# An encoder layer in fp32 by Strassen products: weight sums from GpSimd to VectorE, later attention steps, and sums of activations kept in memory

## The chip, the cores and the metric

The kernel runs on one core of a Trainium2 chip. A core has TensorE (PE in the profile), VectorE (DVE), ScalarE (ACT), GpSimd (POOL) and SyncE (SP), whose queue issues all transfers here. The metric is the device time of one execution in microseconds (us); lower is better.

## What is computed

One encoder layer over 1024 + 512 tokens of width 2048. The linear parts take nearly all of the work:

```python
h = rms_norm(x, pre_g)
q, k, v, g_attn, u, vg, g_gmlp = split(h @ w_in)
a = window_attention(rope(q), rope(k), v, sink) * silu(g_attn)
m = spatial_gating(gelu(u), gelu(vg), ln_g, ln_b, ws, bs) * silu(g_gmlp)
y = concat([a, m]) @ w_out
x = x + rms_norm(y, post_g)
x = x + sigmoid(x @ w_pg) * (p @ w_pe)
```

Attention has 8 heads in 2 groups and looks at blocks of 128 tokens, the own one and its neighbours.

## The kernel before

**Products.** The 1536 tokens are two halves of 768, and the depth of 2048 is two halves of 1024, each of eight tiles of 128. Two column blocks of 128 make a pair. For each pair the four quarter products of a 2 x 2 block product are made from seven products of sums (Strassen), numbered 1 to 7. `A_OF` says which quarters of the activations (A) product `pr` uses and with what sign, `B_OF` the same for the weights. Five of the seven have a sign on either side: two quarters have to be added or subtracted first. Every operand is split into a rounded part and the rest (`split_to`: ScalarE rounds, VectorE subtracts), and each product is three matmuls of 128x384 (`mm3`, lines 174 to 176) for each of 8 depth tiles and 2 token chunks: 48 matmuls, called a pass here.

**Sweeps.** Five sweeps follow each other: a and b (parts of `h @ w_in`), c (the gates), y (`w_out`) and p (`w_pg`), with 8, 6, 8, 8 and 8 pairs. Each goes through the products in the order 3, 5, 7, 1, 4, 2, 6, and in each through its pairs. That is 266 passes. a, b and c have the same A, the normed x, stored as `hn`. Tiles carry the sweep, the product and the pair: `wra7_2_01` is a loaded quarter of a weight, `wta7_2` the split weight, `ara7_3` a quarter of A, `aa7_3` its split, `psa7_2` the product in PSUM.

**Weights.** `make_weights` loads one or two quarters of 128x1024, lets GpSimd add or subtract them into the first (`add(G, ...)`, an instruction of line 155 or 158, the helpers `add` and `sub`), and splits it. **A.** `fetch_operand` loads one or two quarters of 128x768 for the next product and lets VectorE add them; `split_operand` splits it as soon as TensorE is through with the old tile of the same place, so eight splits come in the last pass of a product. For product 7 of sweep a, `x1_normed` makes the sum from tiles that it norms at that time. **Leaving.** `leave_product` adds a product into the accumulators of the pair (VectorE, from PSUM, sometimes ScalarE); only then can the PSUM tile, one of two, take the pass after next. The results then go through rotary steps (`rope`: VectorE and GpSimd), gelu, gates and stores.

**Beside the sweeps.** `embed` makes `p @ w_pe` first, whose 32 products `leave_pe` copies out of PSUM with VectorE. Attention runs as 24 jobs in between (`attention`, half of them in sweep b, half in c): scores `s`, exponentials, transposes `t` of the probabilities `p`, their split `pt`, the output `o`. Spatial gating (`mixing`) lies between the halves.

**Order.** Each engine runs its instructions in the order in which the program issues them. `Line` sets this order: every job is a generator, `yield us` says when it wants to go on, counted on a clock that TensorE's planned time moves (`line.spend`), and between TensorE's steps the jobs that are due issue their instructions. A larger number after `yield` puts what follows later in every queue; nothing waits for a time on the chip. The SP queue is in order too: a store that waits holds the loads behind it.

```python
heapq.heappush(self.jobs, (max(self.now - 1.5, due) + wait, c, gen))
```

Of the kernel before, what the change touches and what calls it, by code (L numbers as in the profile page):

```python
# [9 lines left out]
F32 = mybir.dt.float32  # L10
# [89 lines left out]
def tile_encoder_layer(ctx: ExitStack, tc: tile.TileContext, xT, pT, wall, pre_g, post_g, sink,  # L100
# [69 lines left out]
    def halves(t):  # L170
        return t.rearrange("p (c x) -> p c x", c=2)
# [40 lines left out]

    weights, raw, operands, passes = {}, {}, {}, [0]

    def make_weights(j, sw, pr, i):

        nm = f"{sw.name}{pr}_{i}"
        sign, *quarters = B_OF[pr]
        rs = []
        for kh, n in quarters:  # L220
            r = wrp.tile([P, 1024], F32, tag="wr", name=f"wr{nm}_{n}{kh}")
            load_w(r, sw.pairs[i][n][0], kh)
            rs.append(r)
        yield 9.0
        if sign:
            (add if sign > 0 else sub)(G, rs[0], rs[0], rs[1])
            yield 3.5
        yield from when(lambda: passes[0] >= j - 2)
        w = wtp.tile([P, 2, 1024], F32R, tag="wt", name=f"wt{nm}")
        yield from split_to(rs[0], w[:, 0, :], w[:, 1, :])  # L230
        weights[j] = w

    def fetch_operand(s, sw, pr, k):

        nm = f"{sw.name}{pr}_{k}"
        if s == 1:
            yield from when(lambda: x_stored[0] > 8 + k)
        sign, *quarters = A_OF[pr]
        rs = []
        for pool, tag, (th, kh) in zip((arp, wk), ("ar", "wk"), quarters):  # L240
            r = pool.tile([P, HT], F32, tag=tag, name=f"ar{nm}_{th}{kh}")
            load(r, sw.a[th][kh][k])
            rs.append(r)
        if sign:
            yield 9.0
            (add if sign > 0 else sub)(V, rs[0], rs[0], rs[1])
        raw[s, k] = rs[0]

    def split_operand(s, sw, pr, k):
        yield from when(lambda: (s, k) in raw)  # L250
# [143 lines left out]

    def leave_pe(j, h, ps):
        o = arp.tile([P, HT], F32, tag="ar", name=f"pe{j}_{h}")
        V.tensor_copy(out=halves(o), in_=ps[:, :, 0:CH])
        yield 1.6
        store(pe_d[j][h], o)

# [178 lines left out]
    def attend_qk(g, n, into):  # L579
        b0, b1 = span_of(n)  # L580
        w = (b1 - b0) * P
        nm = f"{g}_{n}"
        h, off = n // HB, (n % HB) * P
        r = [work(f"aq{nm}"), work(f"ak{nm}")]
        load(r[0][:, 0:512].rearrange("p (i t) -> p i t", i=4),
             q_d[g][h][:, :, off:off + P].rearrange("i p t -> p i t"))
        load(r[1][:, 0:w], k_d[g][:, b0 * P:b1 * P])
        yield 9.0
        q = four(f"qs{nm}", [P, 2, 512], F32R)
        ks = four(f"ks{nm}", [P, 2, 512], F32R)  # L590
        nc.scalar.activation(q[:, 0, :], r[0][:, 0:512], AF.Copy)
        nc.scalar.activation(ks[:, 0, 0:w], r[1][:, 0:w], AF.Copy)
        yield 0.8
        sub(V, q[:, 1, :], r[0][:, 0:512], q[:, 0, :].bitcast(F32))
        yield 0.6
        sub(V, ks[:, 1, 0:w], r[1][:, 0:w], ks[:, 0, 0:w].bitcast(F32))
        yield 3.0
        into.append((q, ks))

    def attend_v(g, n, into):  # L600
# [11 lines left out]
    def attend(g, n, got):  # L612

        b0, b1 = span_of(n)
        m0 = (b0 - n + 1) * P
        nb = b1 - b0
        w = nb * P
        nm = f"{g}_{n}"
        h, off = n // HB, (n % HB) * P
        yield from when(lambda: got)  # L620
        q, ks = got.pop()
        mx = small.tile([P, 4], F32, tag="mx", name=f"mx{nm}")
        sm = small.tile([P, 4], F32, tag="sm", name=f"sm{nm}")
        es = small.tile([P, 4], F32, tag="es", name=f"es{nm}")
        gv = []
        line.spawn(attend_v(g, n, gv), 1.0)
        ss, ps_ = [], []

        def reduce(i):
            hd = 4 * g + i  # L630
            p = pp.tile([P, 3 * P], F32, tag="p", name=f"p{nm}_{i}")
            V.tensor_tensor_reduce(out=p[:, 0:w], in0=ss[i][:, 0:w], in1=mask_sb[:, m0:m0 + w],
                                   op0=ALU.add, op1=ALU.min, scale=-SCALE,
                                   scalar=nsink[:, hd:hd + 1], accum_out=mx[:, i:i + 1])
            ps_.append(p)

        def expo(i):
            nc.scalar.activation(ps_[i][:, 0:w], ps_[i][:, 0:w], AF.Exp, scale=-1.0, bias=mx[:, i:i + 1],
                                 accum_out=sm[:, i:i + 1])

        for i in range(6):
            if i < 4:
                ss.append(side(f"s{nm}_{i}"))
                mm3(ss[i][:, 0:w], [q[:, x, i * P:(i + 1) * P] for x in range(2)],
                    [ks[:, x, 0:w] for x in range(2)], True, True, w / 2400. + 0.0133)
            if 1 <= i < 5:
                reduce(i - 1)
            if i >= 2:
                expo(i - 2)
            yield 1.0  # L650
        add(V, es, mx, sink_sb[:, 4 * g:4 * g + 4])
        yield 0.3
        nc.scalar.activation(es, es, AF.Exp)
        yield 0.6
        add(V, sm, sm, es)
        V.reciprocal(out=sm, in_=sm)
        yield 0.6
        for i in range(4):
            nc.scalar.activation(ps_[i][:, 0:w], ps_[i][:, 0:w], AF.Copy, scale=sm[:, i:i + 1])
        yield 4.6  # L660
        pts = {}

        def turn(b):
            tp = side(f"t{nm}_{b}")
            for i in range(4):
                nc.tensor.transpose(tp[:, i * P:(i + 1) * P], ps_[i][:, b * P:(b + 1) * P], ident)
            line.spend(0.43)
            yield 0.4
            pt = pts[b] = four(f"pt{nm}_{b}", [P, 2, 512], F32R)
            yield from split_to(tp, pt[:, 0, :], pt[:, 1, :], 0.9)  # L670

        def weigh(b):
            mm3(o, [vs[:, x, b * P:(b + 1) * P] for x in range(2)],
                [pts[b][:, x, :] for x in range(2)], b == 0, b == nb - 1, 0.2266)

        yield from turn(0)
        yield from turn(1)
        yield from when(lambda: gv)
        vs = gv[0]
        yield 2.0  # L680
        o = side(f"o{nm}")
        weigh(0)
        if nb > 2:
            yield from turn(2)
            yield 2.0
        for b in range(1, nb):
            weigh(b)
        yield 0.8
        t = work(f"ao{nm}")
        nc.scalar.activation(t[:, 0:512], o, AF.Copy)  # L690
        yield 1.5
        store(at_d[g][h][:, :, off:off + P].rearrange("i p t -> p i t"),
              t[:, 0:512].rearrange("p (i t) -> p i t", i=4))
        attended.add((g, n))
# [128 lines left out]
    def x1_normed(k):  # L823
# [9 lines left out]
        if k >= 8:  # L833
            sub(V, r, r, t)
            raw[2, k - 8] = r
        store(hn[1][k // 8][k % 8], t)

    for k in range(KT):
        along("a", 3, k // 2, x1_squares(k), 4.0 * (k % 2))
# [156 lines left out]
```

## Time and profile before

| | us |
|---|---|
| median of 3 runs | 2557.67 (2557.42 to 2560.88) |
| the profiled execution | 2555.26 |
| its span, first to last instruction | 2553.5 |
| TensorE busy | 2483.7 |
| VectorE busy | 1731.8 |
| ScalarE busy | 966.0 |
| GpSimd busy | 708.1 |

Transfers move 645.97 MB, nearly all by one queue. A wait in the profile is named by the engine that waits, the tile and line of the waiting instruction, and behind `<-` what ended last before it began. A stretch 50:125 is from 50 to 125 us after the first instruction. The granted clock is TensorE's, 1.00 being 2.4 GHz.

### The profile page before, as it was taken

How to read it: one execution, taken by the hardware profiler on the slowest of the kernel's cores; microseconds unless marked ns; L12 is line 12 of the kernel's file. 1: busy time of each engine (PE TensorE's matmuls, PEld its weight loads, DVE VectorE, ACT ScalarE, POOL GpSimd, SP SyncE). 2: the span in 40 equal slices, each digit the busy share in tenths (PEclk: the TensorE clock that was granted, in tenths of full speed). 3: DMA queues.
4: the chain of work that ended last, by engine and by line, in shares of the span. 5: the costliest groups of instructions: out<-in, count | busy, mean ns of one | idle time of the engine just before them, and what ended most of it. 6: DMA issues, size and time to landing. Idle time of an engine off the chain costs nothing.

```text
span 2553.5 us, 36547 instructions
## 1 busy us (share of the span) xinstructions
PE 2483.7 (97%) x14268; PEld 2448.7 (96%) x14268; DVE 1731.8 (68%) x1903; ACT 966.0 (38%) x1386; POOL 708.1 (28%) x300
## 2 busy tenths in 40 slices
PE   7999999999999999999998899999999999999999
PEld 7898999999989999999998899999999999999998
DVE  7659566866676767667767665556577976757775
ACT  3243222224775543333546742332233333322421
POOL 0254334454022102301221013203220331433444
PEclk9999999999999999999999999999999999999999
DMA  8957776667566688878656577567577988879985
GB/s 292 387 197 262 249 238 230 225 211 263 195 225 212 180 270 293 303 248 300 200 173 209 187 273 280 219 215 250 170 245 257 342 313 305 302 251 301 325 315 208
DMA packets 372397, 645.97 MB, mean 253 GB/s; under 512 B 29312, under 2 KB 212096, under 8 KB 372224
## 3 DMA queue, kind: packets, MB, share of 16 engines
q1 hardware_dynamic: 372224, 643.63, 73.9%
q8 instruction: 112, 1.84, 0.3%
q14 instruction: 61, 0.50, 0.1%
HBM read 533.43 MB, written 110.10 MB: 252 GB/s over the span
## 4 chain that ended last, share of the span: by engine, by line
PE 80%; DVE 9%; ACT 4%; issue 3%; DMA 3%; POOL 1%; SPq 1%; DVEq 0%; POOLq 0%; ACTq 0%
PE psy L175 6%; PE psy L176 6%; PE psy L174 6%; PE psp L175 6%; PE psp L176 6%; PE psp L174 6%; PE psc L176 4%; PE psc L174 4%; PE psc L175 4%; PE psa L175 4%; PE psa L176 4%; PE psa L174 4%; PE psb L175 4%; PE psb L176 4%; PE psb L174 4%
## 5 line engine op out<-in xcount | busy, mean ns | idle before, releaser
L174 PE MATMUL psa<-aa,wta 128*128 128x384 f32 x896 | 302.3, 337 | 5.7 <-DVE oa L155 3.8
L175 PE MATMUL psa<-aa,wta 128*128 128x384 f32 x896 | 301.7, 337 | 6.0 <-DVE aa L158 5.9
L176 PE MATMUL psa<-aa,wta 128*128 128x384 f32 x896 | 301.1, 336 | 5.8 <-DVE wta L158 5.8
L174 PE MATMUL psc<-ac,wtc 128*128 128x384 f32 x896 | 305.5, 341 | 0.0
L174 PE MATMUL psp<-ap,wtp 128*128 128x384 f32 x896 | 300.5, 335 | 3.2 <-ACT ap L166 2.6
L175 PE MATMUL psp<-ap,wtp 128*128 128x384 f32 x896 | 300.5, 335 | 2.4 <-DVE ap L158 2.4
L175 PE MATMUL psc<-ac,wtc 128*128 128x384 f32 x896 | 301.4, 336 | 0.3 <-DVE ac L158 0.3
L176 PE MATMUL psc<-ac,wtc 128*128 128x384 f32 x896 | 300.7, 336 | 0.0
L176 PE MATMUL psp<-ap,wtp 128*128 128x384 f32 x896 | 299.9, 335 | 0.0
L174 PE MATMUL psy<-ay,wty 128*128 128x384 f32 x896 | 299.6, 334 | 0.0
L176 PE MATMUL psy<-ay,wty 128*128 128x384 f32 x896 | 299.3, 334 | 0.0
L175 PE MATMUL psy<-ay,wty 128*128 128x384 f32 x896 | 299.3, 334 | 0.0
L174 PE MATMUL psb<-ab,wtb 128*128 128x384 f32 x672 | 231.2, 344 | 0.5 <-DVE ua L155 0.5
L175 PE MATMUL psb<-ab,wtb 128*128 128x384 f32 x672 | 226.4, 337 | 2.7 <-DVE ab L158 2.7
L176 PE MATMUL psb<-ab,wtb 128*128 128x384 f32 x672 | 226.0, 336 | 0.0
L175 PEld LDWEIGHTS psa<-aa,wta 128*128 128x128 f32 x896 | 169.3, 189 | 8.4 <-DVE aa L158 8.3
L174 PEld LDWEIGHTS psa<-aa,wta 128*128 128x128 f32 x896 | 169.5, 189 | 6.7 <-issue 4.1
L176 PEld LDWEIGHTS psa<-aa,wta 128*128 128x128 f32 x896 | 169.5, 189 | 6.1 <-DVE wta L158 6.1
L174 PEld LDWEIGHTS psp<-ap,wtp 128*128 128x128 f32 x896 | 168.6, 188 | 4.0 <-ACT ap L166 2.9
L175 PEld LDWEIGHTS psp<-ap,wtp 128*128 128x128 f32 x896 | 168.7, 188 | 3.9 <-DVE ap L158 3.6
L175 PEld LDWEIGHTS psc<-ac,wtc 128*128 128x128 f32 x896 | 169.2, 189 | 1.6 <-DVE ac L158 1.0
L174 PEld LDWEIGHTS psc<-ac,wtc 128*128 128x128 f32 x896 | 169.5, 189 | 0.5
(257 smaller groups left out, 5429.8 us busy)
## 6 DMA issues: line engine op xcount, KB each, us to landing
wrc<-wall SPq DMA_DIRECT2D x96, 512.0 KB, 6.5
arb<-h SPq DMA_DIRECT2D x96, 384.0 KB, 5.9
arc<-h SPq DMA_DIRECT2D x96, 384.0 KB, 6.0
wry<-wall SPq DMA_DIRECT2D x72, 512.0 KB, 6.2
wrp<-wall SPq DMA_DIRECT2D x72, 512.0 KB, 6.8
arp<-x SPq DMA_DIRECT2D x88, 384.0 KB, 6.5
wra<-wall SPq DMA_DIRECT2D x60, 512.0 KB, 5.9
ara<-h SPq DMA_DIRECT2D x80, 384.0 KB, 5.9
```

The lines of the kernel that those rows point to most:

```text
L174: nc.tensor.matmul(ps, lhsT=l[0], rhs=r[0], start=start, stop=False)
L175: nc.tensor.matmul(ps, lhsT=l[0], rhs=r[1], start=False, stop=False)
L176: nc.tensor.matmul(ps, lhsT=l[1], rhs=r[0], start=False, stop=stop)
```

## The change

It does four things. `make_weights` adds or subtracts weight quarters on VectorE (`V`) and not on GpSimd (`G`), and counts 1.6 us and not 3.5 for it. The sums of A that sweep a makes (five products, eight tiles of 128x768 each) are stored to memory (`sum_d`), by `fetch_operand` or, for product 7, by `x1_normed`, and sweeps b and c load such a sum where they loaded two quarters and added them. `leave_pe` copies its first half with ScalarE. In the attention, what follows the split of q and k comes 1.0 later, what follows the scaling of the probabilities 1.0 later, and the two places before the output's matmuls 1.2 later.

```diff
--- before.py
+++ after.py
@@ -212,6 +212,8 @@
 
     weights, raw, operands, passes = {}, {}, {}, [0]
 
+    sum_d = {pr: [scratch(f"sum{pr}_{k}", [P, HT]) for k in range(8)] for pr in A_OF if A_OF[pr][0]}
+
     def make_weights(j, sw, pr, i):
 
         nm = f"{sw.name}{pr}_{i}"
@@ -223,8 +225,8 @@
             rs.append(r)
         yield 9.0
         if sign:
-            (add if sign > 0 else sub)(G, rs[0], rs[0], rs[1])
-            yield 3.5
+            (add if sign > 0 else sub)(V, rs[0], rs[0], rs[1])
+            yield 1.6
         yield from when(lambda: passes[0] >= j - 2)
         w = wtp.tile([P, 2, 1024], F32R, tag="wt", name=f"wt{nm}")
         yield from split_to(rs[0], w[:, 0, :], w[:, 1, :])
@@ -236,6 +238,11 @@
         if s == 1:
             yield from when(lambda: x_stored[0] > 8 + k)
         sign, *quarters = A_OF[pr]
+        if sign and sw.name in "bc":
+            r = arp.tile([P, HT], F32, tag="ar", name=f"ar{nm}")
+            load(r, sum_d[pr][k])
+            raw[s, k] = r
+            return
         rs = []
         for pool, tag, (th, kh) in zip((arp, wk), ("ar", "wk"), quarters):
             r = pool.tile([P, HT], F32, tag=tag, name=f"ar{nm}_{th}{kh}")
@@ -245,6 +252,9 @@
             yield 9.0
             (add if sign > 0 else sub)(V, rs[0], rs[0], rs[1])
         raw[s, k] = rs[0]
+        if sign and sw.name == "a":
+            yield 1.5
+            store(sum_d[pr][k], rs[0])
 
     def split_operand(s, sw, pr, k):
         yield from when(lambda: (s, k) in raw)
@@ -394,7 +404,10 @@
 
     def leave_pe(j, h, ps):
         o = arp.tile([P, HT], F32, tag="ar", name=f"pe{j}_{h}")
-        V.tensor_copy(out=halves(o), in_=ps[:, :, 0:CH])
+        if h:
+            V.tensor_copy(out=halves(o), in_=ps[:, :, 0:CH])
+        else:
+            nc.scalar.activation(halves(o), ps[:, :, 0:CH], AF.Copy)
         yield 1.6
         store(pe_d[j][h], o)
 
@@ -594,7 +607,7 @@
         sub(V, q[:, 1, :], r[0][:, 0:512], q[:, 0, :].bitcast(F32))
         yield 0.6
         sub(V, ks[:, 1, 0:w], r[1][:, 0:w], ks[:, 0, 0:w].bitcast(F32))
-        yield 3.0
+        yield 4.0
         into.append((q, ks))
 
     def attend_v(g, n, into):
@@ -657,7 +670,7 @@
         yield 0.6
         for i in range(4):
             nc.scalar.activation(ps_[i][:, 0:w], ps_[i][:, 0:w], AF.Copy, scale=sm[:, i:i + 1])
-        yield 4.6
+        yield 5.6
         pts = {}
 
         def turn(b):
@@ -677,12 +690,12 @@
         yield from turn(1)
         yield from when(lambda: gv)
         vs = gv[0]
-        yield 2.0
+        yield 3.2
         o = side(f"o{nm}")
         weigh(0)
         if nb > 2:
             yield from turn(2)
-            yield 2.0
+            yield 3.2
         for b in range(1, nb):
             weigh(b)
         yield 0.8
@@ -834,6 +847,9 @@
             sub(V, r, r, t)
             raw[2, k - 8] = r
         store(hn[1][k // 8][k % 8], t)
+        if k >= 8:
+            yield 1.5
+            store(sum_d[7][k - 8], r)
 
     for k in range(KT):
         along("a", 3, k // 2, x1_squares(k), 4.0 * (k % 2))
```

How the built order changes is shown at three places, all on VectorE. In each, the first excerpt is of the kernel before and the second of the changed one.

Sweep a's start, product 3, around the split of pass 2's weight (`wta3_2`); `ara5_0` to `ara5_2` are sums of A for product 5, `aa3_6` is a split of A:

```order
L158 TENSOR_TENSOR aa3_6_1060<-x0_6_345,aa3_6_1060 128x768
L155 TENSOR_TENSOR ara5_0_00_1065<-ara5_0_00_1065,ara5_0_01_1067 128x768
L155 TENSOR_TENSOR ara5_1_00_1101<-ara5_1_00_1101,ara5_1_01_1103 128x768
L158 TENSOR_TENSOR wta3_2_1173<-wra3_2_10_1042,wta3_2_1173 128x1024
L158 TENSOR_TENSOR wta3_3_1184<-wra3_3_10_1076,wta3_3_1184 128x1024
L155 TENSOR_TENSOR ara5_2_00_1137<-ara5_2_00_1137,ara5_2_01_1139 128x768
```

The changed kernel at the same place:

```order
L158 TENSOR_TENSOR aa3_6_1100<-x0_6_385,aa3_6_1100 128x768
L158 TENSOR_TENSOR wra3_2_10_1082<-wra3_2_10_1082,wra3_2_11_1084 128x1024
L155 TENSOR_TENSOR ara5_0_00_1105<-ara5_0_00_1105,ara5_0_01_1107 128x768
L158 TENSOR_TENSOR wra3_3_10_1116<-wra3_3_10_1116,wra3_3_11_1118 128x1024
L158 TENSOR_TENSOR wta3_2_1199<-wra3_2_10_1082,wta3_2_1199 128x1024
L158 TENSOR_TENSOR wta3_3_1212<-wra3_3_10_1116,wta3_3_1212 128x1024
L155 TENSOR_TENSOR ara5_1_00_1141<-ara5_1_00_1141,ara5_1_01_1143 128x768
```

The subtractions of the weights of passes 2 and 3 now stand in the row, and the split of `wta3_2` stands ahead of the sum `ara5_1` and not behind it.

The start of sweep p, product 3, while sweep y's last passes leave (`uy_7`); `x7_0` is the last tile of A that the first pass needs, `ap3_7` its split, and `accy1` sums squares for the next norm:

```order
L158 TENSOR_TENSOR wtp3_1_18468<-wrp3_1_10_18352,wtp3_1_18468 128x1024
L158 TENSOR_TENSOR ap3_5_18477<-x5_0_18266,ap3_5_18477 128x768
L158 TENSOR_TENSOR ap3_6_18487<-x6_0_18335,ap3_6_18487 128x768
L155 TENSOR_TENSOR uy_7_15104<-uy_7_15104,psy6_7_18407 128x768
L862 SCALAR_TENSOR_TENSOR y7_0_18403<-y7_0_18403,post_sb_105,rb_y0_17445 128x768
L155 TENSOR_TENSOR x7_0_18404<-x7_0_18404,y7_0_18403 128x768
L155 TENSOR_TENSOR accy1_17381<-accy1_17381,sqyy15_1_18509 128x768
L158 TENSOR_TENSOR ap3_7_18526<-x7_0_18404,ap3_7_18526 128x768
L158 TENSOR_TENSOR wtp3_2_18551<-wrp3_2_10_18423,wtp3_2_18551 128x1024
```

The changed kernel at the same place:

```order
L158 TENSOR_TENSOR wtp3_1_18292<-wrp3_1_10_18192,wtp3_1_18292 128x1024
L158 TENSOR_TENSOR ap3_3_18298<-x3_0_17968,ap3_3_18298 128x768
L158 TENSOR_TENSOR ap3_4_18309<-x4_0_18037,ap3_4_18309 128x768
L158 TENSOR_TENSOR ap3_5_18318<-x5_0_18106,ap3_5_18318 128x768
L158 TENSOR_TENSOR ap3_6_18327<-x6_0_18175,ap3_6_18327 128x768
L155 TENSOR_TENSOR uy_7_14944<-uy_7_14944,psy6_7_18247 128x768
L878 SCALAR_TENSOR_TENSOR y7_0_18243<-y7_0_18243,post_sb_145,rb_y0_17285 128x768
L158 TENSOR_TENSOR wrp3_2_10_18263<-wrp3_2_10_18263,wrp3_2_11_18265 128x1024
L155 TENSOR_TENSOR x7_0_18244<-x7_0_18244,y7_0_18243 128x768
L155 TENSOR_TENSOR accy1_17221<-accy1_17221,sqyy15_1_18349 128x768
L158 TENSOR_TENSOR ap3_7_18366<-x7_0_18244,ap3_7_18366 128x768
L158 TENSOR_TENSOR wtp3_2_18377<-wrp3_2_10_18263,wtp3_2_18377 128x1024
```

A subtraction for pass 2's weight has come in between `y7_0` and `x7_0`, and the split of `wtp3_1` stands further ahead of `ap3_6`.

A stretch of even work, sweep a's product 1, pass 2 of which leaves PSUM with two adds (`va_2`, `ua_2`):

```order
L158 TENSOR_TENSOR wta1_4_2985<-wra1_4_00_2890,wta1_4_2985 128x1024
L155 TENSOR_TENSOR va_2_1881<-va_2_1881,psa1_2_2940 128x768
L155 TENSOR_TENSOR ua_2_1281<-ua_2_1281,psa1_2_2940 128x768
L440 SCALAR_TENSOR_TENSOR xb2_2938<-xb2_2938,pre_sb_104,rb_x1_1823 128x768
L158 TENSOR_TENSOR wta1_5_3053<-wra1_5_00_2955,wta1_5_3053 128x1024
```

The changed kernel at the same place:

```order
L155 TENSOR_TENSOR wra1_4_00_2954<-wra1_4_00_2954,wra1_4_11_2956 128x1024
L158 TENSOR_TENSOR wta1_4_3040<-wra1_4_00_2954,wta1_4_3040 128x1024
L155 TENSOR_TENSOR va_2_1929<-va_2_1929,psa1_2_3004 128x768
L155 TENSOR_TENSOR ua_2_1324<-ua_2_1324,psa1_2_3004 128x768
L453 SCALAR_TENSOR_TENSOR xb2_3002<-xb2_3002,pre_sb_144,rb_x1_1871 128x768
L155 TENSOR_TENSOR wra1_5_00_3019<-wra1_5_00_3019,wra1_5_11_3021 128x1024
L158 TENSOR_TENSOR wta1_5_3106<-wra1_5_00_3019,wta1_5_3106 128x1024
```

The sums of two weight quarters for `wta1_4` and `wta1_5` (`wra1_4`, `wra1_5`) have come in, each directly ahead of the split of the same weight.

## Rows read from the trace of the kernel before

**Rows 1.** The page's busy times of the engines, share of the span, instructions.
```profile
PE 2483.7 (97%) x14268; PEld 2448.7 (96%) x14268; DVE 1731.8 (68%) x1903; ACT 966.0 (38%) x1386; POOL 708.1 (28%) x300
```

**Rows 2.** TensorE's waits: us in total, times, longest us.
```profile
PE o L175 <- DVE pt L158: 8.0, 5, 3.9
...
PE t L666 <- ACT p L659: 7.7, 20, 1.8
...
PE pspe L174 <- DVE pe L397: 5.9, 3, 3.3
...
PE psa L176 <- DVE wta L158: 5.8, 1, 5.8
...
PE s L175 <- DVE ks L158: 5.3, 5, 1.8
...
PE o L174 <- ACT pt L166: 2.2, 1, 2.2
```

**Rows 3.** Busy us and instructions by stretch, granted clock, transfers.
```profile
core 0: us, PE busy (x) PEld busy (x) DVE busy (x) ACT busy (x) POOL busy (x), PEclk, DMA share, GB/s
...
50.00:125.00 75.00, 65.92 (x352) 64.55 (x351) 52.46 (x52) 18.68 (x22) 19.09 (x8) 0.91 0.98 359
...
125.00:200.00 75.00, 74.15 (x431) 73.27 (x430) 38.41 (x32) 32.66 (x42) 38.27 (x18) 1.00 0.60 198
...
200.00:275.00 75.00, 67.38 (x371) 66.05 (x370) 64.67 (x49) 19.65 (x23) 36.89 (x14) 0.95 0.87 300
...
525.00:625.00 100.00, 95.53 (x545) 93.58 (x545) 64.01 (x73) 31.00 (x48) 49.42 (x26) 0.98 0.71 237
...
625.00:900.00 275.00, 268.41 (x1542) 258.82 (x1540) 187.55 (x296) 175.89 (x317) 45.23 (x19) 0.99 0.66 209
...
1350.00:1475.00 125.00, 108.76 (x586) 100.60 (x585) 85.40 (x124) 85.47 (x138) 12.10 (x5) 0.97 0.58 194
...
2050.00:2100.00 50.00, 46.12 (x256) 44.70 (x255) 37.55 (x35) 15.99 (x20) 14.77 (x6) 0.97 0.84 309
...
2300.00:2500.00 200.00, 199.12 (x1149) 198.80 (x1148) 150.24 (x133) 62.70 (x73) 81.16 (x32) 1.00 0.90 311
```

**Rows 4.** Timeline, VectorE and GpSimd, 2064 to 2078 us: start, us.
```profile
2064.27 0.96 DVE L158 TENSOR_TENSOR ap<-x,ap 128x768 fp32r<-128x768 f32 x1
...
2066.48 2.76 POOL L158 TENSOR_TENSOR wrp<-wrp,wrp 128x1024 f32<-128x1024 f32 x1 [4.60 <-DMA wrp<-wall]
...
2066.89 3.17 DVE L158 TENSOR_TENSOR ap<-x,ap 128x768 fp32r<-128x768 f32 x1
...
2073.95 2.98 POOL L158 TENSOR_TENSOR wrp<-wrp,wrp 128x1024 f32<-128x1024 f32 x1 [4.70 <-DVE wtp L158]
...
2074.59 3.15 DVE L158 TENSOR_TENSOR ap<-x,ap 128x768 fp32r<-128x768 f32 x1
```

**Rows 5.** Groups of instructions: count, busy us, mean ns, idle before them.
```profile
L155 POOL TENSOR_TENSOR wrp<-wrp,wrp 128x1024 f32<-128x1024 f32 x24 | 60.6, 2526 | 85.3 <-DMA wrp<-wall 85.3
...
L158 DVE TENSOR_TENSOR wty<-wry,wty 128x1024 fp32r<-128x1024 f32 x56 | 88.6, 1582 | 24.5 <-ACT wty L166 24.5
...
L155 DVE TENSOR_TENSOR arb<-arb,arb 128x768 f32<-128x768 f32 x24 | 23.4, 974 | 1.5 <-DMA arb<-h 1.5
...
L397 DVE COPY pe<-pspe 128x768 f32<-128x768 f32 x32 | 30.5, 953 | 8.1 <-PE pspe L176 7.0 <-DMA wra<-wall 1.1
...
L260 ACT ACTIVATE ua<-psa 128x768 f32<-128x768 f32 x8 | 6.5, 810 | 19.2 <-PE psa L176 19.2
```

**Rows 6.** Timeline, GpSimd and VectorE, 110 to 117 us.
```profile
110.13 2.36 POOL L158 TENSOR_TENSOR wra<-wra,wra 128x1024 f32<-128x1024 f32 x1 [5.33 <-DMA wra<-wall]
...
114.02 1.41 DVE L155 TENSOR_TENSOR ara<-ara,ara 128x768 f32<-128x768 f32 x1 [7.55 <-DMA ara<-h]
...
115.35 1.21 DVE L158 TENSOR_TENSOR wta<-wra,wta 128x1024 fp32r<-128x1024 f32 x1
```

## The prediction

> **What bounds the kernel now.** Read the busy times first: TensorE is busy 2483.7 of 2553.5 us, VectorE 68%, GpSimd 28% [rows 1]. So TensorE sets the end, and only the 69.8 us in which it stands still, and stretches in which it runs at its lower clock, can be won. The table by stretches says where they lie [rows 3]. Idle time is a stretch's width less TensorE's busy time; the clock's share is its width times what the granted clock lacks of 1.00 (full is 2.4 GHz, and a stretch at 1.2 GHz counts half). This gives 9.1 + 6.8 us in 50:125, 7.6 + 3.8 in 200:275, 4.5 + 2.0 in 525:625, 6.6 + 2.8 in 625:900, 16.2 + 3.8 in 1350:1475 and 3.9 + 1.5 in 2050:2100: 47.9 us of idle time and 20.7 of clock. Elsewhere TensorE hardly waits, and what the change adds there has to stay under a pass, 48 matmuls: 200 us / 1149 x 48 = 8.36 us in the stretch 2300:2500 [rows 3]. Last, TensorE's own waits by releaser [rows 2]: the attention's steps (o, t, s) wait 8.0 + 7.7 + 5.3 + 2.2 = 23.2 us, almost always for VectorE or for ScalarE behind it. VectorE is thus the engine that is late where TensorE waits, though it is 68% busy on average.
>
> **Why VectorE is late.** A split of an operand takes 0.96 us. Two splits of the same tile and shape take 3.17 and 3.15 us, and each began while GpSimd ran a weight sum: from 2066.48 for 2.76 us, and from 2073.95 for 2.98 us [rows 4]. The first split ends at 2070.06, 0.82 us after GpSimd's end: VectorE did not share, it stood still until GpSimd was through. The group of all splits of sweep y's weights averages 1.58 us, where 1.21 is the time of one alone [rows 5, 6].
>
> **The weight sums move to VectorE.** There are five signed products of seven and 38 pairs, so 190 sums. GpSimd loses 190 x about 2.6 us [rows 5], some 500 of its 708. VectorE gains 190 x 1.21 = 230 us (a subtraction of two 128x1024 tiles took 1.21 [rows 6]). Three things come off it: 80 sums of A at 0.97 (`arb`) = 78 us [rows 5], 16 copies out of PSUM at 0.95 = 15 us [rows 5], and the standstill behind sums. The last I bound by 0 and 190 x 2.2 us (3.17 - 0.96) and take at 120: not every sum meets a blocked instruction. VectorE ends at 1732 + 230 - 78 - 15 - 120, about 1750 us: as busy as before, but without 2 us holes, and a weight is summed in 1.2 instead of 2.6 us.
>
> What it adds is a wait on VectorE. In 72 of the 190 places the new order puts a weight's split directly behind its sum, as in the third pair of the order's excerpts, and the split needs ScalarE's rounding in between. ScalarE's copies of a smaller tile take 0.81 [rows 5]; scaled to 1024 columns that is 1.08, about 1.2 with both hand-overs. Behind the waiting split stand the adds that empty PSUM for the pass after next. In the densest steady stretch, 2300:2500, VectorE has 150.2 us in 24 passes, 6.26 a pass. With 5/7 x (1.21 + 1.2) = 1.72 more it has 7.98, under 8.36 even if nothing of the standstill goes. So I cost this at little: 3 us in all for new waits, two the size of the one that I leave at sweep p's start, with 0 and 13 us as ends.
>
> **Start, 50:125.** TensorE waits 5.8 us for the split of pass 2's weight [rows 2], which begins at 115.35 because the second operand sum before it waits for its load until 114.02. In the new order the split stands ahead of that sum, behind the subtraction for pass 3, whose load had landed at 110.13 [rows 6]. It then ends at 110.13 + 1.21 + 1.21 = 112.55 instead of 116.56: 4.0 us. The longest wait for a copy out of PSUM, 3.3 us [rows 2], which the move of half the copies to ScalarE should end, brings no more: transfers run at 98% in 50:125, so TensorE would only reach the later wait sooner. ScalarE's 16 copies, 13 us, are hidden beside TensorE; without that cover they would cost 0.81 us each. Against it stand the new stores: 40 of 384 KB, the first eight between the loads of this stage. At 359 GB/s each takes 1.1 us, 8.8 for eight; in 125:200 the share is down to 60%, so I take 4.0, with a loss of 4.8 (4.0 - 8.8) as the other end. The SP queue is in order, and a store waits for its sum; queued behind it are loads of later weights. The other 32 stores lie in stretches with spare transfer time. In sweeps b and c, 80 loads less take 31 MB off.
>
> **Sweep a, 200:275.** VectorE is busy 64.7 of 75 us. Four sums of 7's weights fall here. Each gives back up to 2.2 and costs 1.21, so 1.0 a piece: 4 of the 11.4 us, the ends 0 and 11.4. The rotary steps stay on GpSimd and go on blocking.
>
> **525:625.** GpSimd is busy 49.4 of 100 us with rotary steps and sums in one queue; a sum on VectorE no longer queues behind them. I take 4 of 6.5, ends 0 and 6.5. Here a rule of the Trainium skill speaks against the change: SBUF — State Buffer, section "Who interferes with whom", says that a VectorE instruction with two SBUF inputs contends with a GpSimd instruction that reads SBUF, and that the later one blocks entirely. By it the sums, now such instructions, are themselves held by the rotary steps; this term would be 1 and the total 3 us later, inside the forecast's own range. The pair of splits above agrees with the rule; for a sum on VectorE no run here shows it.
>
> **Attention, 625:900 and 1350:1475.** The allowances grow by 1.0 (before s), 1.0 (before t) and twice 1.2 us (before o): TensorE does other passes meanwhile, at no cost but a later end of the job, and the built order has the last job end in sweep c's second-last product, ahead of the one that needs it. They take at most 1.0 from each of 5 waits of s, 1.0 from each of some 5 jobs with waits of t (20 rows, four in a job), 1.2 from each of 6 of o: 17 us. What is longer than its allowance (3.9, 2.2, 1.8, 1.8) is about what one or two standstills of 2.2 make. I take 16 of the 23.2 and 4 of the clock's 6.6: 20 us, with 0 and 29.8 as ends.
>
> **Start of sweep p, 2050:2100.** Both standstills of 2.2 us lie ahead of the last splits; one sum of 1.21 comes in there (second pair of excerpts). VectorE reaches the last split about 3 us sooner; 4 of 5.4 us.
>
> **Sum.** 4 + 4 + 4 + 20 + 4 - 3 = 33 us. The profiled execution took 2555.26, so 2522; the median of the runs lies 2.4 above it, so **2524 us**.
>
> **Rivals.**
> 1. *Attention stays late.* ScalarE, with its table loads, could be what holds the steps, and the allowances only move the waits. For it: t waits for ScalarE's p in all 20 rows [rows 2]. Against: ScalarE is itself behind VectorE's row there. That term falls from 20 to 6: 2538.
> 2. *Everything is cleared.* All losses of the five later stretches go, 11.4 + 6.5 + 9.4 + 20.0 + 5.4, and 4.0 at the start: 57 us, 2501. Against: the hand-overs still bring eight splits in one pass.
> 3. *Slower: late weights hold VectorE.* On GpSimd a sum that waited for its load held only sums. On VectorE it holds PSUM's emptying and the splits. Place: sweep p and the end of y, where transfers run at 84 to 90% [rows 3]. With a wait of w a sum, a pass takes 7.98 + 0.71 w on VectorE, so it decides from w = 0.5 us; at 2.4 us (a GpSimd sum's whole length lost, the nearest row) it is 1.3 us a pass, over some 54 passes 72 us: 2596. Against: loads are issued 9 us ahead in the program, and its order leaves that as it was.
>
> **Chances.** Forecast 0.60 (2512 to 2536), attention stays late 0.16, all cleared 0.08, late weights 0.10; the other 0.06 is gains and new waits that cancel. Within 0.2%, 5 us, a measurement of this kernel can't tell from no change. So faster 0.84, same 0.06, slower 0.10. The range 2503 to 2548 holds the forecast, the first rival with 10 us on top for the stores' worse end, and stops short of the last.
>
> **What would show it.** GpSimd near 210 us with 110 instructions; VectorE near 1750 with 1997; the weight splits' mean near 1.21; TensorE's idle time near 45 us; pass 2's weight split ending about 4 us sooner; waits for o, t and s together under 8 us. Wrong would be: VectorE idle on weight loads for over 100 us (rival 3), t's waits unchanged (rival 1), a granted clock under 0.90 in 100:200 (the stores).

## The result and the profile after

The changed kernel takes **2497.25 us** (median of four runs, 2496.87 to 2498.64); the kernel before, beside it on the same chip, 2557.55 (2556.95 to 2560.88). The ratio is 0.9763, 95% interval 0.9746 to 0.978. The gain is 60 us where 33 were forecast, and the time lies under the range (2503). The profiled execution took 2496.87 us, its span is 2495.1.

The page's busy times after, in the form of [rows 1]:

```profile
PE 2460.8 (99%) x14268; PEld 2437.8 (98%) x14268; DVE 1704.0 (68%) x1997; ACT 980.6 (39%) x1400; POOL 221.6 (9%) x110
```

TensorE stands still for 2495.1 - 2460.8 = 34.3 us where it stood 69.8. It is also busy 22.9 us less at the same 14268 matmuls: a matmul that runs at the lower clock counts as busy time, and so does a short wait inside a group, since the records overlap (in the rows of transposes further down, 256 of 273 ns each fill 38.9 us). The gain of 58.4 us in the span is thus 35.5 of idle time and 22.9 of busy time.

TensorE's own waits after, answering [rows 2] (engine, tile, line, what ended the wait; us in total, times, longest):

```profile
PE pspe L174 <- ACT pe L410: 4.3, 2, 3.3
PE psa L176 <- DVE wta L158: 3.2, 1, 3.2
...
PE psa L175 <- DVE aa L158: 2.4, 2, 1.5
PE o L175 <- DVE pt L158: 2.1, 3, 1.0
...
PE o L174 <- ACT pt L166: 1.1, 1, 1.1
...
PE s L175 <- DVE ks L158: 0.5, 1, 0.5
PE t L679 <- ACT p L672: 0.4, 2, 0.2
```

The attention's steps (o, t, s) wait 4.1 us, before 23.2. The wait for pass 2's weight has fallen from 5.8 to 3.2.

The stretches of [rows 3] after. The same work stands up to 58 us earlier now, so a stretch shows the idle time and clock of that part of the program, not the same instructions:

```profile
core 0: us, PE busy (x) PEld busy (x) DVE busy (x) ACT busy (x) POOL busy (x), PEclk, DMA share, GB/s
50.00:125.00 75.00, 69.81 (x387) 68.20 (x386) 50.13 (x49) 26.17 (x33) 8.07 (x4) 0.98 1.01 367
...
200.00:275.00 75.00, 70.67 (x397) 70.12 (x397) 63.30 (x55) 20.28 (x24) 17.15 (x7) 0.98 1.00 350
...
525.00:625.00 100.00, 100.00 (x588) 99.64 (x587) 63.09 (x83) 38.06 (x65) 26.10 (x13) 1.00 0.63 207
625.00:900.00 275.00, 272.45 (x1587) 265.12 (x1587) 177.21 (x286) 181.32 (x317) 0.00 (x0) 1.00 0.58 177
...
1350.00:1475.00 125.00, 123.67 (x722) 120.52 (x721) 79.33 (x135) 87.89 (x148) 0.00 (x0) 1.00 0.63 210
...
2050.00:2100.00 50.00, 50.00 (x290) 50.00 (x289) 30.70 (x32) 17.12 (x20) 0.00 (x0) 1.00 0.79 298
```

The groups of weight splits in sweeps y and p, answering [rows 5] (count; busy us, mean ns; idle before), and a split of `x` at sweep p's start, answering [rows 4] (GpSimd ran nothing from 2005 to 2030 us):

```profile
L158 DVE TENSOR_TENSOR wtp<-wrp,wtp 128x1024 fp32r<-128x1024 f32 x56 | 90.2, 1611 | 23.5 <-ACT wtp L166 23.5
...
L158 DVE TENSOR_TENSOR wty<-wry,wty 128x1024 fp32r<-128x1024 f32 x56 | 68.5, 1224 | 42.7 <-ACT wty L166 42.6
```

```profile
2012.81 0.95 DVE L158 TENSOR_TENSOR ap<-x,ap 128x768 fp32r<-128x768 f32 x1
```

Sweep y's splits took 1582 ns before. Sweep p's still have GpSimd's last adds beside them. In the table of stretches, from 525 us on hardly anything is left; what remains lies in the start and around 200 to 275 us.

**Where the gain arose.** The best measure is the start of the same pass in both traces: how much sooner it begins, and by how much that grows from one place of the program to the next. The columns of the two tables below are six pieces of the program: the *start* (up to the first pass of sweep a's product 5, 167.7 us in the kernel before), *a5-7* (up to the fifth pass of product 7, 283.1), *a rest* (up to the second pass of sweep b, 605.6), *attention* (up to sweep y, 1601.9), *y-p3* (up to sweep p's product 5, 2145.9) and *end* (up to the last pass, 2538.7).

| us | start | a5-7 | a rest | attention | y-p3 | end |
|---|---|---|---|---|---|---|
| forecast | 4.0 | 4 | 4 | 20 | 4 | -3 (new waits) |
| measured | 6.4 | 4.6 | 10.1 | 31.4 | 3.9 | 1.7 |

### The profile page after: what moved, and what is told of

Read it like the earlier page. It is cut to its first block, busy times and chain, and to the rows that moved or that the text cites. A ratio compares the mean times of both kernels' runs of the same rounds, so it can differ in the third digit from the quotient of the medians.

```text
span 2495.1 us, 36057 instructions
## 1 busy us (share of the span) xinstructions
PE 2460.8 (99%) x14268; PEld 2437.8 (98%) x14268; DVE 1704.0 (68%) x1997; ACT 980.6 (39%) x1400; POOL 221.6 (9%) x110
## 4 chain that ended last, share of the span: by engine, by line
PE 90%; DVE 3%; DMA 2%; ACT 2%; issue 1%; POOL 0%; SPq 0%; DVEq 0%; ACTq 0%
PE psp L175 6%; PE psp L176 6%; PE psp L174 6%; PE psy L175 6%; PE psy L174 6%; PE psy L176 6%; PE psc L175 6%; PE psc L174 6%; PE psc L176 6%; PE psa L176 5%; PE psa L175 5%; PE psa L174 5%; PE psb L175 4%; PE psb L176 4%; PE psb L174 4%; PE t L679 1%
```

## The experiments

Theory 1: the main loss was VectorE's standstill behind GpSimd's sums. Theory 2: the attention's steps were due too early, whatever GpSimd did. Theory 3: the stored sums relieved VectorE and the transfers. Theory 4 came later. The medians and gains by piece (gain over the kernel before, from one profiled execution each; these scatter between kernels that should agree there, in the start by up to 5 us and in a5-7 by up to 3, so that only larger differences are read; the kernels were timed in six groups, each beside the kernel before, whose median lay between 2556.16 and 2560.35):

| kernel | median us (lowest to highest) | start | a5-7 | a rest | attention | y-p3 | end |
|---|---|---|---|---|---|---|---|
| changed | 2497.25 (2496.87 to 2498.64) | 6.4 | 4.6 | 10.1 | 31.4 | 3.9 | 1.7 |
| e1 changed, sums on GpSimd | 2534.9 (2532.7 to 2539.07) | 3.4 | 2.1 | -1.1 | 18.3 | -2.4 | 0.2 |
| e2 before, sums on VectorE | 2515.22 (2514.17 to 2516.8) | 7.8 | 2.9 | 10.1 | 14.3 | 3.8 | 1.7 |
| e3 before, later attention | 2540.94 (2530.08 to 2544.28) | 0.5 | -1.3 | 0.1 | 18.1 | -0.1 | -1.5 |
| e4 changed, old attention | 2513.33 (2512.8 to 2515.78) | 8.9 | 2.2 | 10.1 | 15.1 | 3.9 | 1.6 |
| e5 before, stored sums | 2555.2 (2549.52 to 2561.53) | 0.2 | 1.1 | -1.6 | 0.4 | -0.4 | -1.0 |
| e6 changed, no stored sums | 2500.4 (2498.99 to 2501.69) | 7.4 | 4.7 | 10.1 | 28.2 | 3.9 | 1.7 |
| e7 before, copies on ScalarE | 2557.71 (2551.12 to 2563.17) | 2.7 | 1.1 | -1.0 | 2.2 | 0.0 | -0.9 |
| e8 changed, old copies | 2498.18 (2497.55 to 2498.65) | 6.3 | 2.9 | 10.1 | 31.5 | 3.9 | 1.6 |
| e9 changed, idle GpSimd adds | 2528.52 (2527.51 to 2530.65) | 8.6 | -4.4 | 2.5 | 27.6 | -6.2 | -3.6 |
| e10 changed, idle GpSimd fills | 2497.26 (2496.61 to 2501.85) | 3.6 | 2.3 | 10.1 | 31.5 | 3.9 | 1.7 |
| e11 changed, no GpSimd sums | 2492.98 (2489.88 to 2495.97) | 8.2 | 9.8 | 10.1 | 31.4 | 3.9 | 1.7 |
| e12 e11, attention later still | 2503.2 (2498.34 to 2504.43) | 8.3 | 8.4 | 10.1 | 23.5 | -0.8 | 1.6 |
| e13 e4, idle GpSimd adds | 2546.61 (2541.79 to 2551.51) | 7.4 | -4.4 | 2.5 | 9.0 | -7.3 | -3.8 |
| e14 changed, sums counted 3.5 | 2509.22 (2502.7 to 2510.21) | 0.3 | 2.5 | 10.0 | 29.6 | 0.7 | 1.6 |

### Two parts of the change, each taken back and each alone (e1 to e4)

The edit of e1, and the reverse of it in the kernel before for e2:

```diff
-            (add if sign > 0 else sub)(V, rs[0], rs[0], rs[1])
-            yield 1.6
+            (add if sign > 0 else sub)(G, rs[0], rs[0], rs[1])
+            yield 3.5
```

> The changed kernel with its 190 weight sums back on GpSimd and their old allowance of 3.5; the stored sums, the copies and the later attention stay. Theory 1 (VectorE standing still while a GpSimd sum runs was the main loss): most of the 60 us comes back, about 2535 us; TensorE waits for o, t and s 10 us or more, the mean of sweep y's weight splits is again near 1.58 us. Theory 2 (the attention's steps were simply due too early): only the stretches outside the attention lose, about 2518 us, and o, t and s stay near 4 us. Theory 3 (the stored sums relieved VectorE and the transfers): under 2510 us.

> The kernel before with one change, the weight sums on VectorE (allowance 1.6). Theory 1: about 2512 us, since without the standstills the old allowances of the attention nearly do. Theory 2: about 2530 us, the attention's waits for o, t and s stay at 20 us or more. Theory 3: no gain or a loss, 2550 us or more, because VectorE then has the 230 us of weight sums and still the 78 us of sums of A.

The four longer allowances in the kernel before (e3), and taken back in the changed one (e4):

```diff
         sub(V, ks[:, 1, 0:w], r[1][:, 0:w], ks[:, 0, 0:w].bitcast(F32))
-        yield 3.0
+        yield 4.0
...
-        yield 4.6
+        yield 5.6
         pts = {}
...
         vs = gv[0]
-        yield 2.0
+        yield 3.2
...
             yield from turn(2)
-            yield 2.0
+            yield 3.2
```

> The kernel before with one change, the four longer allowances in the attention. Theory 1: about 2545 us, o, t and s fall from 23 to some 15 us, since a standstill of 2.2 us and more is longer than the 1.0 to 1.2 us added. Theory 2: about 2528 us, o, t and s under 6 us.

> The changed kernel with the attention's old allowances. Theory 1: about 2505 us, o, t and s at 8 us or less. Theory 2: about 2525 us, o, t and s back at 20 us or more.

Measured: 2534.9, 2515.22, 2540.94 and 2513.33 us. The sums alone gain 41.7 us (2556.93 beside it), the later attention alone 16.0; taken back, they cost 37.7 and 16.1. The two add up to nearly all of the 60. Theory 1 gives the larger part, and the smaller part is theory 2's: neither was right alone. Their signs lie between them too: o, t and s together wait 9.2 us in e3 and 13.6 in e4. In e1 one sign of theory 1 is missing, since sweep y's weight splits average 1.31 us and not 1.58. In the attention both count, 14.3 and 18.1 us, and 14.3 + 18.1 is about the 31.4 of both together. TensorE's waits there in e2 (sums alone) and e3 (later steps alone):

```profile
PE t L666 <- ACT p L659: 5.0, 17, 1.0
PE o L175 <- DVE pt L158: 4.4, 4, 1.6
...
PE o L174 <- ACT pt L166: 2.4, 2, 2.2
...
PE s L175 <- DVE ks L158: 0.8, 1, 0.8
```

```profile
PE o L175 <- DVE pt L158: 6.2, 4, 2.3
...
PE o L174 <- ACT pt L166: 2.1, 2, 1.1
...
PE t L666 <- ACT p L659: 0.9, 5, 0.2
```

Against [rows 2], moving the sums clears s (5.3 to 0.8) and leaves many short waits of t (17, the longest 1.0). The later steps clear t and s and leave the long waits of o. So the two overlap in s and differ in t and o: in the list of waits they take 10.6 and 14.0 us, and 19.1 together. That the gains in time add up so nearly is in part chance; what the list does not hold is busy time, told below.

### The stored sums and the copies (e5 to e8)

For e5 and e6 all lines with `sum_d` are put into the kernel before or taken out of the changed one; for e7 and e8 the branch in `leave_pe`.

> The kernel before with one change, the stored sums of A. Theory 1 (transfers and VectorE's 78 us of sums are hidden, except in the start): a loss at the start up to 5 us, none later, so 2555 to 2560 us; VectorE near 1640 us busy with no gain in time. Theory 3 (they relieve VectorE in the attention, where TensorE waits for it): 2550 us or less.

> The changed kernel without the stored sums: sweeps b and c load two quarters and add them again, VectorE near 1785 us busy. Theory 1: 2493 to 2499 us, at the start some 2 to 5 us better than the changed kernel (no stores between the loads there), later passes equal. Theory 3: 2505 us or more.

> The kernel before with one change, half of the copies out of PSUM at the start on ScalarE. By the prediction (transfers bound the start, TensorE only reaches the later wait sooner): within 1 us of before, about 2557 us. By what the passes of the changed kernel show (sweep a's first pass begins 3.8 us earlier): about 2554 us.

> The changed kernel with all copies at the start on VectorE. By the prediction: 2496 to 2498 us, no change. By the first pass of sweep a, which begins 3.8 us earlier than before in the changed kernel: about 2501 us.

Measured: 2555.2 (ratio 0.999, 0.9977 to 1.0003), 2500.4, 2557.71 (1.0006, 0.9988 to 1.0023) and 2498.18 us. Theory 3 falls as a main cause: alone, the stored sums do nothing that can be measured; in the changed kernel they are worth 3.2 us, all of it in the attention (28.2 without them, 31.4 to 31.5 in four kernels with them). So theory 1's expectation for e6, at most 2499 us with later passes equal, was missed as well. The copies let sweep a's first pass begin 3.5 to 3.8 us sooner, and by product 5 no more than 0.1 (changed kernel) to 2.7 us (the kernel before) is left: TensorE reaches the next wait sooner, as the prediction said. The expectation of 2501 us for e8, which took the first pass for the end, was wrong.

### GpSimd instructions that do nothing (e9, e10)

```diff
             (add if sign > 0 else sub)(V, rs[0], rs[0], rs[1])
             yield 1.6
+            add(G, rs[1], rs[1], rs[1])
```

For e10 the added line is `G.memset(rs[1], 0.0)`, twice.

> The changed kernel, and behind each of its 190 weight sums an add on GpSimd of the used quarter to itself (128x1024, two inputs in memory on chip, some 2.6 us); nobody reads its result, and nothing of the reference is left out. Theory 1 (a VectorE instruction with two such inputs stands still while a GpSimd instruction that reads on-chip memory runs): 2515 to 2530 us, weight splits that begin inside such an add take 2.5 us and more. Theory 2 (GpSimd's sums were late or queued, VectorE was not held): 2497 to 2502 us.

> As the run with the GpSimd adds, but with two fills of the same quarter with zeros in place of each add: GpSimd writes on-chip memory and reads none. Theory 1 in its narrow form (only GpSimd instructions that read count): 2497 to 2502 us, splits at 1.22 us. If any GpSimd instruction holds VectorE: as the run with the adds, scaled by the fills' length. Theory 2: 2497 to 2502 us in both.

Measured: 2528.52 and 2497.26 us. 190 adds whose result nobody reads cost 31 us; 380 fills in their place cost nothing. The page's busy times of e9 and of e10:

```profile
PE 2474.8 (98%) x14268; PEld 2442.6 (97%) x14268; DVE 1878.0 (74%) x1997; ACT 978.8 (39%) x1400; POOL 657.3 (26%) x300
```

```profile
PE 2464.3 (99%) x14268; PEld 2440.7 (98%) x14268; DVE 1691.7 (68%) x1997; ACT 981.0 (39%) x1400; POOL 579.4 (23%) x490
```

VectorE has the same 1997 instructions and is busy 1878.0 - 1691.7 = 186 us longer beside the adds: that is its standstill. Beyond the changed kernel's 221.6 us, GpSimd is busy another 436 us with the adds and 358 with the fills. One weight split beside an add in e9, and one beside a fill in e10 (timeline: start, us):

```profile
1688.24 2.49 POOL L155 TENSOR_TENSOR wry<-wry 128x1024 f32<-128x1024 f32 x1 [79.22 <-DVE wry L155]
...
1689.24 2.57 DVE L158 TENSOR_TENSOR wty<-wry,wty 128x1024 fp32r<-128x1024 f32 x1 [0.26 <-ACT wty L166]
```

```profile
1676.00 0.95 POOL L231 MEMSET wry<- 128x1024 f32 x1
...
1676.01 1.23 DVE L158 TENSOR_TENSOR wty<-wry,wty 128x1024 fp32r<-128x1024 f32 x1 [0.26 <-ACT wty L166]
```

The first split ends 1.08 us after the add (1691.81 against 1690.73), so it did its work only when GpSimd was through. The second runs as if it were alone. This settles the mechanism for these two kinds: VectorE is held by a GpSimd add, which reads, and not by a fill, which only writes. The two differ in arithmetic and length as well; no run takes these apart from the reading. The losses of e9 lie in sweeps a and p (9.0 + 7.6 in sweep a, 10.1 + 5.3 in y, p), only 3.8 in the attention.

### Which part the attention paid for (e13, e14)

That left a gap: moving the sums back costs the attention 13.1 us (31.4 - 18.3), idle adds 3.8. Theory 4: it is the sums' place in the order and their length that cost the attention.

> The changed kernel with the attention's old allowances, and behind each weight sum the idle add on GpSimd (nobody reads its result, nothing of the reference is left out). Compared with the run without the later attention, 2513 us, of which some 20 of its 44 us gain lie in the attention. Theory 1 (the standstill is what the attention paid for): the attention loses 12 us or more of these 20, with the 24 us that the adds cost in sweeps a and p about 2550 us. Theory 4 (the sums' length and place on GpSimd cost the attention): it loses 6 us or less there, about 2540 us.

> The changed kernel with the weight sums on VectorE, but counted as 3.5 us as they were on GpSimd, so each split stands 1.9 us later in the order. Theory 1: no change, 2495 to 2500 us, the attention's gain stays 36 us. Theory 4: 2505 us or more, the attention loses 10 us or more.

e13 is e4 with the line of e9; e14 is the changed kernel with `yield 3.5` in place of 1.6. Measured: 2546.61 and 2509.22 us. In e14 the attention loses 1.8 us, so the place is not it, and that half of theory 4 falls. In e13 the attention loses 6.1 (15.1 to 9.0) by the table. The two expectations count sweep b's first pass, which the table leaves to *a rest*, as part of the attention; by their count it loses 8.7 (20.1 to 11.4), between the 6 of theory 4 and the 12 of theory 1, and neither is confirmed. Of e13's 48 instructions that stood still in the attention (longer by over 0.15 us than the median of their kind, beside a GpSimd instruction), 33 were weight splits; in the kernel before 9 of 49 were, the others splits of A and steps of the attention. In sum they stood still for 46 us in e13 and 77 in the kernel before, so the idle adds bring back only a part of it. The idle adds start right behind a sum, not when a load lands, and so meet other instructions. That the difference is the remaining loss is argued, not shown; the other half of theory 4, a sum that takes 2.6 us on GpSimd and holds its own split up, was not separated from it.

What e14 does show is the start: it gains 0.3 us there, where the kernels with the changed order gain 3.6 to 8.9. TensorE's longest wait in the start of e14, and VectorE's row around it:

```profile
PE psa L176 <- DVE wta L158: 7.3, 1, 7.3
```

```profile
108.80 1.22 DVE L158 TENSOR_TENSOR wra<-wra,wra 128x1024 f32<-128x1024 f32 x1 [2.13 <-DMA wra<-wall]
112.64 1.51 DVE L155 TENSOR_TENSOR ara<-ara,ara 128x768 f32<-128x768 f32 x1 [2.62 <-DMA ara<-h]
114.07 3.99 DVE L158 TENSOR_TENSOR wta<-wra,wta 128x1024 fp32r<-128x1024 f32 x2
```

The sum of A that waits for its load again stands ahead of the weight's split. The changed kernel's row at the same place:

```profile
107.65 1.23 DVE L158 TENSOR_TENSOR wra<-wra,wra 128x1024 f32<-128x1024 f32 x1 [1.54 <-DMA wra<-wall]
108.80 2.43 DVE L158 TENSOR_TENSOR wta<-wra,wta 128x1024 fp32r<-128x1024 f32 x2
111.51 2.22 DVE L155 TENSOR_TENSOR ara<-ara,ara 128x768 f32<-128x768 f32 x1 [0.29 <-DMA ara<-h]
```

So the start hangs on the number behind `yield`: a counted 1.6 puts the split of pass 2's weight ahead, and the move to VectorE without it gains nothing that can be read there. A sum on GpSimd that counts 1.6 was not run.

### Beyond the change (e11, e12)

In e11 GpSimd's remaining sums and products, 96 instructions, go to VectorE:

```diff
-            mul(G, o[:, s:e], o[:, s:e], c)
+            mul(V, o[:, s:e], o[:, s:e], c)
...
-        add(G, o, o, b)
+        add(V, o, o, b)
...
-            add(G, o, o, x[:, 0:HT])
+            add(V, o, o, x[:, 0:HT])
...
-        yield from accumulate(x_acc[1], k == 0, t, t, G)
+        yield from accumulate(x_acc[1], k == 0, t, t, V)
```

> The changed kernel with the remaining adds and products of GpSimd (rotary steps, the last adds of sweep p, the squares of the second half) on VectorE too, some 85 of the 110 instructions. Theory 1: each costs VectorE 0.95 us and gives back up to 2.6 us where an instruction stood behind it; TensorE's waits in sweep a's products 3 to 7 (1.5 for a split of A, 2.8 for the rotary result) shrink, 2490 to 2497 us, the weight splits' mean is 1.22 us in every sweep. Theory 2 (VectorE, by then the only engine for it, becomes the bound in sweep a): 2500 us or more.

> As the run without GpSimd sums, with the attention's allowances longer again, by 0.6 (before s and before t) and twice 1.0 us (before o). What is left there is 4.1 us of waits for o, t and s. If allowances still pay: 2 to 4 us under the run without GpSimd sums. If the jobs end too late: slower than that run, with a wait in sweep c's last products.

Measured: 2492.98 and 2503.2 us. e11 is 4 us under the changed kernel, and all its runs lie under all of that one's; it is the fastest version here, though the two were not timed side by side and 4 us is 0.2%. Its page and its stretch 200:275:

```profile
PE 2458.4 (99%) x14268; PEld 2435.2 (98%) x14268; DVE 1702.2 (68%) x2093; ACT 979.7 (39%) x1400; POOL 12.6 (1%) x14
```

```profile
200.00:275.00 75.00, 73.34 (x421) 72.50 (x420) 59.68 (x63) 20.14 (x23) 0.00 (x0) 1.00 1.01 362
```

VectorE takes on 96 instructions and is busy 1702.2 us instead of 1704.0: the standstill that ends pays for all of them. In 200:275 it runs 63 instructions in 59.7 us, where it needed 63.3 for 55.

e12 shows the other end of the allowances. Its TensorE in 1460:1480, and what it waits for there:

```profile
1460.00:1480.00 20.00, 10.19 (x43) 7.64 (x43) 17.20 (x30) 12.99 (x27) 0.00 (x0) 0.77 0.39 117
```

```profile
PE s L174 <- ACT ao L703: 4.4, 1, 4.4
PE t L679 <- ACT p L672: 4.1, 1, 4.1
PE o L175 <- DVE pt L158: 1.3, 1, 1.3
```

9.8 us of idle time and a granted clock of 0.77 in one place. One job is not through when the passes of sweep c's product 2 are, and its steps now follow each other with no pass in between, ahead of product 6; in e11 the same job's output begins at 1440.5 us, with three passes of product 2 still to come. A longer allowance is free only while passes are left to lie beside it. Another 4.7 us of e12's loss lie in y-p3, beside no new wait of TensorE: its clock is at the lower level for 10 us there, from 2031 us on, and no run shows why.

## Why the prediction was wrong

The mechanism was right in the main, the direction too; several terms of the sum were too small, the attention's most of all. By the pieces the forecast is 25 us short of 58: 11.4 in the attention, 6.1 in sweep a's rest, 4.7 in new waits that did not come, 2.4 in the start.

- **The standstill.** Bounded by 0 and 190 x 2.2 us and taken at 120. e2 measures it: 1731.8 + 190 x 1.22 is 1963.6 us for VectorE, and its page shows 1793.4, so 170 went on balance. e9 against e10 gives 186. VectorE ends at 1704 and not near 1750.

```profile
PE 2470.4 (98%) x14268; PEld 2441.0 (97%) x14268; DVE 1793.4 (71%) x2093; ACT 972.9 (39%) x1386; POOL 225.4 (9%) x110
```

- **Start, 4.0 against 6.4.** The step was right: the split of pass 2's weight moves ahead of the sum of A, and e14, whose wait for it is 7.3 us against 3.2, shows that this order is the gain. The split ends at 110.01 and not 112.55, since the load of pass 3's quarter had landed by 107.65, 2.5 us sooner than the 110.13 of [rows 6] on which the prediction built. The copies are worth nothing much there, as forecast, but the wait that their move should end is still 3.3 us long, now for ScalarE's copy. The stores cost about 1 us by one profile (7.4 without them), which is within the scatter, and not the 8.8 of the worse end.
- **Sweep a's rest, 4 against 10.1.** I had counted 4 of 6.5 us in 525:625 and nothing around it. All waits went, in 375:525 too (1.9 us idle before, none after), and at sweep b's first pass (5.0 of the 10.1). The rule of the Trainium skill that I weighed here (SBUF — State Buffer, section "Who interferes with whom") holds, but its price does not show: sums on VectorE do stand still behind rotary steps (2.87 us instead of 1.22 in the rows below, at 227 us; 1.68 and 2.02 for two in 525:625), and the changed kernel still has no idle time in 525:625. By it this term would have been 1. The rule speaks against leaving the rotary steps on GpSimd, and e11, which moves them, gains 5.2 us more than the changed kernel around product 7, and e12 3.8.

```profile
226.17 2.62 POOL L161 TENSOR_TENSOR oa<-oa,cos 128x768 f32<-128x768 f32 x1 [5.63 <-DMA ara<-h]
...
227.00 2.87 DVE L155 TENSOR_TENSOR wra<-wra,wra 128x1024 f32<-128x1024 f32 x1
```

- **Attention, 20 against 31.4: the step that failed.** Its upper end of 29.8 was the listed waits of o, t and s plus the clock of two stretches, and the measured value lies above that end. I put the later steps and the moved sums under one ceiling and took two thirds of it. e2 to e4 show two gains, 14.3 and 18.1, that together reach beyond it. The ceiling was too low, because the list of waits isn't all of the loss. From sweep b's second pass to sweep y, the kernel before and the changed one:

```profile
605.00:1602.00 997.00, 973.11 (x5666) 950.08 (x5665) 686.21 (x959) 501.77 (x835) 183.78 (x74) 0.99 0.71 239
```

```profile
584.00:1549.00 965.00, 960.65 (x5663) 945.46 (x5662) 621.76 (x949) 501.63 (x832) 4.00 (x4) 1.00 0.66 214
```

Idle time falls from 23.9 to 4.4 us, but TensorE's busy time falls too, by 12.5 us at nearly the same number of matmuls (5666 and 5663). I had counted 16 us of idle time and 4 of the clock; 19.5 and 12.5 came, so the term was mis-sized most where I had only the clock. The clock is a part of it: before, 10 us of this stretch stand at the lower level, worth 5 us, and after none. Another part sits in the transposes, 256 in either kernel (before, then after):

```profile
L666 PE MATMUL t<-ident,p 128*128 128x128 f32 x256 | 44.2, 282 | 8.0 <-ACT p L659 7.7
```

```profile
L679 PE MATMUL t<-ident,p 128*128 128x128 f32 x256 | 38.9, 273 | 0.4 <-ACT p L672 0.4
```

They were busy 5.3 us longer, on top of the 7.7 of waits that the list shows. Some 2 us more are not traced to one place.

- **Sweep a at 200:275, 4 against 4.6, and the start of sweep p, 4 against 3.9.** Right in place and size, the first only as far as its scatter lets one say.
- **New waits, -3 against none.** VectorE does wait for weight loads now, and TensorE's time shows none of it. Rival 3, late weights that hold VectorE, has its waits and not its price: 0.5 us per sum would be 95 us, and the three largest groups together have 24.2 us, and all of them 32:

```profile
DVE wra L158 <- DMA wra<-wall: 12.9, 8, 6.9
DVE wrp L158 <- DMA wrp<-wall: 7.4, 6, 1.6
DVE wrc L158 <- DMA wrc<-wall: 3.9, 4, 1.1
```

- **The rivals.** "Everything is cleared", 2501 us, was the nearest, and I gave it 0.08 against "the hand-overs still bring eight splits in one pass". They do, and VectorE gets through them in time. "Attention stays late" fell: t's waits went from 7.7 to 0.4.

Of the signs named beforehand, GpSimd near 210 us with 110 instructions (221.6), VectorE's 1997 instructions, waits of o, t and s under 8 (4.1) and an earlier split came in. Idle time came out at 34.3 and not 45. The weight splits' mean is 1.22 us in sweeps b, c and y, but 1.40 in a and 1.61 in p, where GpSimd's remaining steps still hold them; in e11 it is 1.22 in all five.

## What to carry to other kernels

Before work goes to GpSimd, look at what VectorE does meanwhile: an add there held VectorE instructions with two inputs in memory on chip until it ended (e9 against e10), so an engine that looks free at 28% made the busy one late. To bound what clearing a chain of waits can bring, take the stretch's idle time, its clock and the busy time of the short steps against their time when nothing waits; the list of waits alone is too little. An allowance in a hand-made order is free up to the point where a job runs out of passes to lie beside; measure both sides of it.

## What the runs showed of the hardware that was not expected

The rows of before showed VectorE's splits beside GpSimd's sums only, and so did not tell which instructions of either engine count. Fills on GpSimd (0.95 us each for 128x1024) hold nothing: 380 of them left the time at 2497.26 us, and the split in the excerpt of e10 ran in 1.23. VectorE adds with one input in PSUM aren't held either, even beside a GpSimd sum: in the kernel before, 53 that began inside one took 0.94 to 0.96 us each. From the kernel before, sweep y:

```profile
1825.85 2.40 POOL L155 TENSOR_TENSOR wry<-wry,wry 128x1024 f32<-128x1024 f32 x1 [4.50 <-DMA wry<-wall]
...
1826.76 0.95 DVE L155 TENSOR_TENSOR vy<-vy,psy 128x768 f32<-128x768 f32 x1 [4.33 <-PE psy L176]
1827.63 0.95 DVE L155 TENSOR_TENSOR uy<-uy,psy 128x768 f32<-128x768 f32 x1
```

The adds that empty PSUM begin inside the sum and take their usual 0.95 us. This fits with how much GpSimd work could stand beside the products without stopping them, and with the loss falling on the splits. Both findings agree with the rule of the Trainium skill (SBUF — State Buffer, section "Who interferes with whom"), which speaks of a VectorE instruction with two SBUF inputs and of a GpSimd instruction that reads SBUF.
